# A hybrid decoder trunk on one core: norm weights as rows spread by a matmul, token tiles in other buffers, TensorE started on zeros

## The chip, the core and the metric

One core of a Trainium2 chip runs the whole program. The metric is the device time of one execution in microseconds; the profile is of one execution, recorded by the hardware profiler.

## The reference

A trunk of two layers over 1024 tokens of width 1024, in f32, with 256 memory tokens. What the change touches is the preparation: the RMSNorm of the memory tokens with the weights `g_mem`, the RMSNorm of the tokens with the weights `even_norm_g`, and the keys and values of the memory for both layers.

```
def rmsnorm(x, g):
    xf = x.astype(jnp.float32)
    y = xf * lax.rsqrt(jnp.mean(xf * xf, axis=-1, keepdims=True) + EPS)
    return (y * g.astype(jnp.float32)).astype(x.dtype)

mem_n = rmsnorm(mem, g_mem)                       # (256, 1024)
# even layer
h = rmsnorm(x, even_norm_g)                       # (1024, 1024)
proj = h @ w_in                                   # then attention, pooling, memory attention
mk, mv = jnp.split(mem_n @ w_mem_kv, 2, axis=-1)  # the same for the odd layer
```

After it come dilated window attention, pooling, memory attention, gating and an output projection (even layer), a spatial gate, memory attention and an output projection (odd layer), and a last norm.

## The kernel before, in words

Every large product is made in three matmuls of float32r operands: each f32 operand is split into a part `hi` (a copy on ScalarE, L113) and the rest `lo` (a subtraction on VectorE, L114). The projections use a seven-product scheme over blocks (`pair`, L236 is its matmul).

The change lies in the preparation. In program order it is:

- The two memory tiles of 128 tokens are loaded into buffers of the tag `xt` (three of them, L493), the weights `g_mem` are loaded with a broadcast to all 128 partitions into a buffer of the tag `gmb` (one, L496), and the identity for transposes (L497).
- `norm_T` for each memory tile: the square on ScalarE with its sum (L344), mean and epsilon on VectorE (L346), the power -1/2 on GpSimd (L347), the multiply by it and by the weights on VectorE (L372), eight transposes on TensorE (L377) into two PSUM banks (the first of the tag `s`, which has two banks, the other of `tr` or `pv`, one each), and from each bank a `hi` copy on ScalarE (L381) and a `lo` subtraction on VectorE (L382).
- The weights `g_even` are loaded with a broadcast into the same buffer `gmb` (L501).
- `mem_kv(0)` and `mem_kv(1)`: for each of four heads a weight tile is loaded (`mraw`, L505, six buffers) and split, 24 matmuls of 256 columns (L569) make the keys, the copy (L572) and the store (L573) follow; then one token tile is loaded (`xt`, L576) and goes through `norm_T` with `g_even`. Four more weight tiles and 48 matmuls of 512 columns (L402 to L404) make the values (copy L583, store L584). Between the two calls stands the table of rotation angles (`rope_angles`), which writes `sncs`.
- Then four weight tiles of the value projection are loaded into the buffers of the tag `raw` (three, L109), and the rest of the program follows.

All loads and stores go through SyncE's queue, in order. The order of each engine's instructions isn't written by hand: the framework takes the program's order as priority and places what it holds to be ready, when the program is built; so the order on an engine differs from that of the text (the load of L501 was issued behind two of L505 and one of L576). Buffers of one tag are used in turn, and a new use waits until the last reader of the old one is done.

Of the kernel before, what the change touches and what calls it, by code (L numbers as in the profile page):

```python
# [8 lines left out]
F32 = mybir.dt.float32  # L9
F32R = mybir.dt.float32r  # L10
BF = mybir.dt.bfloat16
I32 = mybir.dt.int32
AF = mybir.ActivationFunctionType
# [11 lines left out]
W2 = 10  # L25
# [24 lines left out]
def trunk(ctx, tc, A):  # L50
    nc = tc.nc
    PS = bass.MemoryType.PSUM
    V, S, G, T, D = nc.vector, nc.scalar, nc.gpsimd, nc.tensor, nc.sync

    def pool(name, side="left"):
        st = ExitStack()
        return st, st.enter_context(tc.tile_pool(name=name, bufs=1, side=side, reuse_waits="tile"))

    fix = ctx.enter_context(tc.tile_pool(name="fix", bufs=1))
# [3 lines left out]
    def bank(tag):  # L63
        return psum.tile([128, 512], F32, name=tag, tag=tag, bufs=dict(pj=4, s=2, tr=1, pv=1)[tag])
# [17 lines left out]
    def at(t, off, ap):  # L82
        return bass.AP(tensor=t.tensor, offset=t.offset + off, ap=ap)
# [7 lines left out]
    sncs = fix.tile([128, 2, 128], F32, name="sncs")  # L91
# [15 lines left out]
    def load_raw(src):  # L107
        raw = fix.tile([128, 1024], F32, name="raw", tag="raw", bufs=3)
        D.dma_start(raw, src)  # L109
        return raw  # L110
# [253 lines left out]
    def norm_T(*a):  # L364
        for _ in norm_steps(*a):
            pass
# [29 lines left out]
    def tok512(ps, hi_src, lo_src, chunks, t):  # L396
        ts = slice(t * 128, (t + 1) * 128)
        for k in range(8):
            wh, wl = chunks[k // 2]
            c = k % 2  # L400
            hi, lo = hi_src[k // 4][:, k % 4, ts], lo_src[k // 4][:, k % 4, ts]
            T.matmul(ps, hi, wh[c], start=(k == 0), stop=False)  # L402
            T.matmul(ps, hi, wl[c], start=False, stop=False)  # L403
            T.matmul(ps, lo, wh[c], start=False, stop=(k == 7))  # L404

    def bcast(ap, n, off=0):
        return bass.AP(tensor=ap.tensor, offset=ap.offset + off, ap=[[0, 128], [1, n]])
# [77 lines left out]
    sx, xn = pool("xn", "right")  # L485
# [1 line left out]
    mnh = [pm.tile([128, 4, 256], F32R, name=f"mnh{k}") for k in range(2)]  # L487
    mnl = [pm.tile([128, 4, 256], F32R, name=f"mnl{k}") for k in range(2)]
    mem_t = []
    gb = xn.tile([128, 1024], F32, name="gmb", tag="gmb")  # L490
    for t in range(2):
        m = xn.tile([128, 1024], F32, name="xt", tag="xt", bufs=3)
        D.dma_start(m, A["mem"][t * 128:(t + 1) * 128, :])  # L493
        mem_t.append(m)
        if t == 0:
            D.dma_start(gb, bcast(A["g_mem"], 1024))  # L496
            D.dma_start(ident, A["ident"])  # L497
    for t in range(2):
        norm_T(xn, mem_t[t], gb, mnh, mnl, t)
    gb2 = xn.tile([128, 1024], F32, name="gmb", tag="gmb")  # L500
    D.dma_start(gb2, bcast(A["g_even"], 1024))  # L501

    def m_raw(src):
        raw = p0.tile([128, 1024], F32, name="mraw", tag="mraw", bufs=MR)
        D.dma_start(raw, src)  # L505
        return raw

    def m_w(raw):
        o = []
        for c in range(2):  # L510
            hi = p0.tile([128, 4, 128], F32R, name="mwh", tag="mw", bufs=MW)
            lo = p0.tile([128, 4, 128], F32R, name="mwl", tag="mw", bufs=MW)
            f = "p k c -> p (k c)"
            split(raw[:, c * 512:(c + 1) * 512], hi.rearrange(f), lo.rearrange(f))
            o.append((hi, lo))
        return o

    def m_chunk(raw):
        o = m_w(raw)
        return [[x[q].rearrange("p k c -> p (k c)") for x in o] for q in range(2)]  # L520
# [41 lines left out]
    def mem_kv(l):  # L562
        for h in range(4):
            o = m_w(m_raw(A["kv1k" if l == 0 else "kv2k"][h]))
            ps = bank("pj")
            for k in range(8):
                hi, lo = o[k // 4]
                for w, m in ((hi, mnh), (hi, mnl), (lo, mnh)):
                    T.matmul(ps[:, :256], w[:, k % 4, :], m[k // 4][:, k % 4, :], start=(k == 0 and w is hi and m is mnh),  # L569
                             stop=(k == 7 and w is lo))  # L570
            mt = pm.tile([128, 512], F32, name="mt", tag="mt", bufs=2)
            S.activation(mt[:, :256], ps[:, :256], AF.Copy)  # L572
            D.dma_start(mkv_d[l, :, 0, h * 256:(h + 1) * 256], mt[:, :256])  # L573
            t = TORD[l * 4 + h]
            x = xn.tile([128, 1024], F32, name="xt", tag="xt", bufs=3)
            D.dma_start(x, A["x"][t * 128:(t + 1) * 128, :])  # L576
            norm_T(xn, x, gb2, hTh, hTl, t)
        ch = [m_chunk(m_raw(A["kv1v" if l == 0 else "kv2v"][c])) for c in range(4)]
        for t in range(2):
            ps = bank("pj")  # L580
            tok512(ps, mnh, mnl, ch, t)
            mt = pm.tile([128, 512], F32, name="mt", tag="mt", bufs=2)
            S.activation(mt, ps, AF.Copy)  # L583
            D.dma_start(mkv_d[l, :, 1, t * 512:(t + 1) * 512], mt)  # L584

    TORD = (4, 5, 6, 7, 0, 1, 2, 3)
    open_hT()
    mem_kv(0)
    D.dma_start(smalls, A["smalls"])
    rope_angles()  # L590
    mem_kv(1)
    ch = [chunk(p, A["wev"][c]) for c, p in enumerate((None, None, xn, xn))]
    sm.close()
# [6 lines left out]
    for t in TORD:  # L600
        ps = bank("pj")
# [709 lines left out]
```

## Time and profile before

| what | us |
|---|---|
| median of 3 runs | 1297.51 |
| lowest and highest run | 1295.16 and 1304.29 |
| the profiled execution | 1299.02 |
| its span | 1297.3 |

The span is the time from the first to the last instruction of the profile; the 1.7 us between it and the time of the same execution lie around it. Busy times are of instructions only; a matmul's own duration holds its way through the array, so matmuls that follow each other overlap, and their pace is read from the differences of their starts. L12 is line 12 of the kernel; L113, L114, L236, L344 to L382 are lines of helpers that many parts of the program use.

### The profile page before, as it was taken

Reading aid. Unit: us, or ns where it says so; the run is one execution under the profiler, and the core shown is the slowest. Engines: PE = TensorE matmul, PEld = TensorE weight load, DVE = VectorE, ACT = ScalarE, POOL = GpSimd, SP = SyncE. Lnnn points to the kernel's source line nnn. Section 1 sums busy time; section 2 is a strip of 40 time slices with the busy share of each in tenths; the row PEclk is TensorE's granted clock in tenths of the full one; section 3 lists DMA queues with packets and bytes.
Section 4 is the critical chain, followed back from the end, with each engine's and each line's share of the span. In section 5 each row is a group of like instructions: output and inputs, shape, how many; then the busy total and the mean of one; then the engine's idle time right before and its main releaser. Section 6 shows DMA issues by size and latency. Waiting matters only on the chain.

```text
span 1297.3 us, 17470 instructions
## 1 busy us (share of the span) xinstructions
PE 1255.0 (97%) x6008; PEld 1027.5 (79%) x6008; DVE 1042.8 (80%) x1968; ACT 576.7 (44%) x1155; POOL 48.3 (4%) x51
## 2 busy tenths in 40 slices
PE   6999999999999998999999999999999999999997
PEld 6888778878877776778888887877888877888886
DVE  6998768776776876879988977997878999777976
ACT  6734322232245455447653644632655233244552
POOL 1162000000000000000000001000000000000001
PEclk9999999999999999999999999998999999999999
DMA  7834756576555557633359534523122667239633
GB/s 273 281 98 142 216 189 205 189 241 198 162 161 181 159 172 259 224 114 94 122 177 373 164 114 188 185 90 114 34 83 97 212 217 252 66 106 334 243 112 130
DMA packets 128990, 226.10 MB, mean 174 GB/s; under 512 B 11139, under 2 KB 79363, under 8 KB 128902
## 3 DMA queue, kind: packets, MB, share of 16 engines
q1 hardware_dynamic: 128902, 224.99, 52.3%
q8 instruction: 47, 0.77, 0.3%
q14 instruction: 41, 0.34, 0.1%
HBM read 158.79 MB, written 63.01 MB: 171 GB/s over the span
## 4 chain that ended last, share of the span: by engine, by line
PE 72%; DVE 12%; DMA 10%; issue 3%; ACT 1%; POOL 1%; SPq 1%; DVEq 0%; POOLq 0%; ACTq 0%
PE pj L236 36%; DMA sl<-qk_d 3%; PE pj L954 3%; PE pj L953 3%; PE pj L955 3%; DVE wl L114 2%; PE pj L402 2%; PE pj L403 2%; PE pj L404 2%; PE pv L449 1%; PE pj L569 1%; PE s L430 1%; DMA raw<-in_we_dram 1%; PE s L720 1%; PE s L954 1%
## 5 line engine op out<-in xcount | busy, mean ns | idle before, releaser
L236 PE MATMUL pj<-hTh,wh 128*128 128x512 f32 x544 | 218.0, 401 | 8.7 <-DVE u L249 7.6
L236 PE MATMUL pj<-hTl,wh 128*128 128x512 f32 x544 | 215.1, 395 | 0.0
L236 PE MATMUL pj<-hTh,wl 128*128 128x512 f32 x544 | 214.5, 395 | 0.0
L113 ACT ACTIVATE wh<-sw 128x512 fp32r<-128x512 f32 x136 | 85.9, 632 | 244.6 <-PE pj L236 211.6
L236 PEld LDWEIGHTS pj<-hTh,wh 128*128 128x128 f32 x544 | 102.8, 189 | 36.5 <-DVE u L249 12.4
L113 ACT ACTIVATE wh<-raw 128x512 fp32r<-128x512 f32 x106 | 66.8, 630 | 142.9 <-PE pj L236 134.8
L114 DVE TENSOR_TENSOR wl<-sw,wh 128x512 fp32r<-128x512 f32 x136 | 93.6, 689 | 35.2 <-ACT wh L113 35.2
L236 PEld LDWEIGHTS pj<-hTh,wl 128*128 128x128 f32 x544 | 103.0, 189 | 21.5 <-issue 0.2
L236 PEld LDWEIGHTS pj<-hTl,wh 128*128 128x128 f32 x544 | 103.2, 190 | 19.8 <-issue 0.2
L113 ACT ACTIVATE owh<-raw 128x512 fp32r<-128x512 f32 x84 | 52.3, 628 | 73.8 <-DMA raw<-wt_d 31.5
L114 DVE TENSOR_TENSOR wl<-raw,wh 128x512 fp32r<-128x512 f32 x106 | 73.7, 696 | 9.4 <-ACT wh L113 8.1
L114 DVE TENSOR_TENSOR owl<-raw,owh 128x512 fp32r<-128x512 f32 x84 | 57.7, 691 | 29.1 <-ACT owh L113 28.5
L953 PE MATMUL pj<-owh,oyh 128*128 128x512 f32 x192 | 76.1, 397 | 0.0
L954 PE MATMUL pj<-owl,oyh 128*128 128x512 f32 x192 | 75.8, 395 | 0.0
L955 PE MATMUL pj<-owh,oyl 128*128 128x512 f32 x192 | 75.2, 395 | 0.0
L205 DVE TENSOR_TENSOR wt<-wt 128x256 f32<-128x256 f32 x128 | 51.7, 426 | 11.8 <-DMA wt<-in_wov_dram 5.2
L236 PE MATMUL pj<-t2h,wh 128*128 128x512 f32 x136 | 55.3, 407 | 0.0
L236 PE MATMUL pj<-t2l,wh 128*128 128x512 f32 x136 | 54.3, 399 | 0.0
L236 PE MATMUL pj<-t2h,wl 128*128 128x512 f32 x136 | 54.2, 399 | 0.0
L236 PE MATMUL pj<-t0h,wh 128*128 128x512 f32 x136 | 54.1, 398 | 0.0
L236 PE MATMUL pj<-t0l,wh 128*128 128x512 f32 x136 | 54.1, 398 | 0.0
L236 PE MATMUL pj<-t1l,wh 128*128 128x512 f32 x136 | 53.8, 395 | 0.0
(367 smaller groups left out, 3063.4 us busy)
## 6 DMA issues: line engine op xcount, KB each, us to landing
raw<-in_we_dram SPq DMA_DIRECT2D x44, 512.0 KB
wt_d<-wt SPq DMA_DIRECT2D x24, 512.0 KB
y<-y_d SPq DMA_DIRECT2D x24, 512.0 KB
raw<-wt_d SPq DMA_DIRECT2D x48, 256.0 KB
raw<-in_wo_dram SPq DMA_DIRECT2D x24, 512.0 KB
y_d<-X SPq DMA_DIRECT2D x20, 512.0 KB
qk_d<-X SPq DMA_DIRECT2D x24, 384.0 KB
sl<-qk_d SPq DMA_DIRECT2D x16, 512.0 KB
```

The lines of the kernel that those rows point to most:

```text
L113: S.activation(hi, raw, AF.Copy)
L114: e.tensor_tensor(lo, raw, hi.bitcast(F32), op=OP.subtract)
L205: V.tensor_tensor(tt[:, o, :], tt[:, x, :], tt[:, y, :], op=op)
L236: T.matmul(ps, w[:, k, :], m, start=(start and k == 0 and w is hi and m is B[k][0]), stop=(k == 3 and w is lo), skip_group_check=True)
L402: T.matmul(ps, hi, wh[c], start=(k == 0), stop=False)
L403: T.matmul(ps, hi, wl[c], start=False, stop=False)
L404: T.matmul(ps, lo, wh[c], start=False, stop=(k == 7))
L430: T.matmul(s3[:, a, :], qs[i][:, (t0 + a) * 128:(t0 + a + 1) * 128], kvp[j][:, :256], start=n == 0, stop=n == 2)
L449: T.matmul(pv[:, pr * 256:(pr + 1) * 256], kvp[i][:, 256 + kb * 128:384 + kb * 128], PT[j][:, kb * 256:(kb + 1) * 256], start=(kb == 0 and ...
L953: T.matmul(ps, yh[:, c], wh, start=start, stop=False, skip_group_check=True)
L954: T.matmul(ps, yh[:, c], wl, start=False, stop=False, skip_group_check=True)
L955: T.matmul(ps, yl[:, c], wh, start=False, stop=stop, skip_group_check=True)
```

## The change

The weights of the two norms come as rows of 4 KB into one partition of two buffers of the tag `raw`. A function `spread` multiplies a row by a row of ones (one partition of `sncs`, which is written later by the angles), in two matmuls of 512 columns into two banks of the tag `s`, and ScalarE copies the halves to the buffer `gmb`. A buffer of the tag `w2` is set to zero; `idle(n, tag)` issues n matmuls of 512 columns of these zeros, as bfloat16, into one bank: four ahead of the first spread and four behind it. The token tiles of numbers 0, 2 and 3 are loaded into buffers `raw` instead of `xt`.

```
--- before.py
+++ after.py
@@ -487,18 +487,38 @@
     mnh = [pm.tile([128, 4, 256], F32R, name=f"mnh{k}") for k in range(2)]
     mnl = [pm.tile([128, 4, 256], F32R, name=f"mnl{k}") for k in range(2)]
     mem_t = []
-    gb = xn.tile([128, 1024], F32, name="gmb", tag="gmb")
+
+    zero = fix.tile([128, 512], F32, name="zero", tag="w2", bufs=W2).bitcast(BF)
+    V.memset(zero, 0.0)
+    one = sncs[0:1, 0, :]
+    V.memset(one, 1.0)
+    grow = [fix.tile([128, 1024], F32, name="raw", tag="raw", bufs=3)[0:1, :] for _ in range(2)]
     for t in range(2):
         m = xn.tile([128, 1024], F32, name="xt", tag="xt", bufs=3)
         D.dma_start(m, A["mem"][t * 128:(t + 1) * 128, :])
         mem_t.append(m)
+        D.dma_start(grow[t], at(A[("g_mem", "g_even")[t]], 0, [[1024, 1], [1, 1024]]))
         if t == 0:
-            D.dma_start(gb, bcast(A["g_mem"], 1024))
             D.dma_start(ident, A["ident"])
+
+    def idle(n, tag):
+        ps = bank(tag)
+        for _ in range(n):
+            T.matmul(ps, zero[:, :128], zero[:, :512], start=True, stop=True)
+
+    def spread(row):
+        g = xn.tile([128, 1024], F32, name="gmb", tag="gmb")
+        for c in range(2):
+            ps = bank("s")
+            T.matmul(ps, one, row[:, c * 512:(c + 1) * 512], start=True, stop=True)
+            S.activation(g[:, c * 512:(c + 1) * 512], ps, AF.Copy)
+        return g
+    idle(4, "pj")
+    gb = spread(grow[0])
+    idle(4, "s")
     for t in range(2):
         norm_T(xn, mem_t[t], gb, mnh, mnl, t)
-    gb2 = xn.tile([128, 1024], F32, name="gmb", tag="gmb")
-    D.dma_start(gb2, bcast(A["g_even"], 1024))
+    gb2 = spread(grow[1])
 
     def m_raw(src):
         raw = p0.tile([128, 1024], F32, name="mraw", tag="mraw", bufs=MR)
@@ -572,8 +592,12 @@
             S.activation(mt[:, :256], ps[:, :256], AF.Copy)
             D.dma_start(mkv_d[l, :, 0, h * 256:(h + 1) * 256], mt[:, :256])
             t = TORD[l * 4 + h]
-            x = xn.tile([128, 1024], F32, name="xt", tag="xt", bufs=3)
-            D.dma_start(x, A["x"][t * 128:(t + 1) * 128, :])
+            n = l * 4 + h
+            if n in (0, 2, 3):
+                x = load_raw(A["x"][t * 128:(t + 1) * 128, :])
+            else:
+                x = xn.tile([128, 1024], F32, name="xt", tag="xt", bufs=3)
+                D.dma_start(x, A["x"][t * 128:(t + 1) * 128, :])
             norm_T(xn, x, gb2, hTh, hTl, t)
         ch = [m_chunk(m_raw(A["kv1v" if l == 0 else "kv2v"][c])) for c in range(4)]
         for t in range(2):
```

## Rows read from the trace of the kernel before

**Rows 1.** The page, part 1: busy us (share of the span) and instructions.

```profile
PE 1255.0 (97%) x6008; PEld 1027.5 (79%) x6008; DVE 1042.8 (80%) x1968; ACT 576.7 (44%) x1155; POOL 48.3 (4%) x51
```

**Rows 2.** Busy time by stretch: length, engines, granted clock, DMA share, GB/s.

```profile
0.00:15.00 15.00, 4.37 (x18) 3.44 (x18) 6.01 (x11) 8.40 (x14) 1.99 (x9) 1.00 0.75 245
15.00:24.30 9.30, 9.30 (x57) 9.21 (x58) 5.81 (x9) 5.24 (x11) 1.10 (x2) 1.00 0.80 294
24.30:60.00 35.70, 35.40 (x246) 31.88 (x244) 34.63 (x89) 25.64 (x51) 4.13 (x5) 1.00 0.85 296
8.00:10.00 2.00, 1.69 (x8) 1.57 (x8) 0.41 (x2) 1.32 (x3) 0.00 (x1) 1.00 1.04 424
```

**Rows 3.** The chain of waits, 0 to 60 us: start, us, what.

```profile
14.99 5.28 PE pj L569 x23
...
44.91 2.84 PE pj L569 x24
...
56.11 4.49 DMA raw<-in_wev_dram
```

**Rows 4.** Timeline of TensorE, 16 to 22 us: start, us, engine, line, what.

```profile
16.01 0.41 PE L569 MATMUL pj<-mnh,mwl 128*128 128x256 f32 x1
...
16.22 0.41 PE L569 MATMUL pj<-mnh,mwh 128*128 128x256 f32 x1
...
20.06 0.90 PE L377 MATMUL s<-ident,h 128*128 128x128 f32 x4
...
20.80 0.60 PE L377 MATMUL tr<-ident,h 128*128 128x128 f32 x4
...
21.83 0.29 PE L569 MATMUL pj<-mnh,mwl 128*128 128x256 f32 x1
...
21.95 0.28 PE L569 MATMUL pj<-mnh,mwh 128*128 128x256 f32 x1
```

**Rows 5.** Timeline of ScalarE and VectorE, 0 to 22 us.

```profile
4.90 1.06 ACT L344 ACTIVATE h<-xt 128x1024 f32<-128x1024 f32 x1 [2.82 <-DMA xt<-in_mem_dram]
...
6.97 1.29 DVE L372 SCALAR_TENSOR_TENSOR h<-xt,rs,gmb 128x1024 f32<-128x1024 f32 x1 [0.73 <-POOL rs L347]
...
8.58 1.06 ACT L344 ACTIVATE h<-xt 128x1024 f32<-128x1024 f32 x1 [2.53 <-DMA xt<-in_mem_dram]
...
10.59 1.28 DVE L372 SCALAR_TENSOR_TENSOR h<-xt,rs,gmb 128x1024 f32<-128x1024 f32 x1 [0.67 <-POOL rs L347]
...
14.25 0.68 DVE L382 TENSOR_TENSOR mnl<-s,mnh 128x512 fp32r<-128x512 f32 x1
...
16.44 1.28 DVE L372 SCALAR_TENSOR_TENSOR h<-xt,rs,gmb 128x1024 f32<-128x1024 f32 x1 [0.91 <-DMA gmb<-in_g_even_dram]
...
21.63 0.69 DVE L382 TENSOR_TENSOR hTl<-s,hTh 128x512 fp32r<-128x512 f32 x1 [0.53 <-ACT hTh L381]
```

**Rows 6.** Timeline of SyncE's queue, 0 to 12 us.

```profile
0.80 0.39 SPq L493 DMA_DIRECT2D xt<-in_mem_dram  x1
...
2.18 0.43 SPq L493 DMA_DIRECT2D xt<-in_mem_dram  x1
...
3.62 0.50 SPq L505 DMA_DIRECT2D mraw<-in_kv1k_dram  x1
11.90 0.33 SPq L501 DMA_DIRECT2D gmb<-in_g_even_dram  x1
```

**Rows 7.** Timeline, 395 to 400 us: a copy, a PSUM copy, f32 weight loads.

```profile
395.44 0.69 DVE L763 COPY PT<-tr 128x512 f32<-128x512 f32 x1 [1.99 <-PE tr L760]
...
398.10 0.60 ACT L771 ACTIVATE n<-pv 128x512 f32<-128x512 f32 x1
...
399.48 0.19 PEld L791 LDWEIGHTS tr<-ps,wp 128*128 128x128 f32 x1 [0.24 <-DVE st L690]
...
399.91 0.19 PEld L791 LDWEIGHTS tr<-ps,wp 128*128 128x128 f32 x1 [0.24 <-issue]
```

**Rows 8.** Line L1164, matmuls with two partitions: shortest, median, longest ns.

```profile
L1164 PE MATMUL pv<-rh,lh x16: 270/394/578, 892.7 to 897.6; 2*128 2x128 f32 x16
```

## The prediction

> **What bounds the kernel now.** I began with the page's busy times: TensorE has work in 97% of the span, VectorE in 80%, ScalarE in 44% [rows 1]. So only a stage in which TensorE is not the limit, or runs slowly, can give time back. The diff touches nothing after the preparation, so I read the table of busy time by stretch for the first 65 us [rows 2]. TensorE works 4.37 of the first 15.00 us, all of the next 9.30, 35.40 of 35.70 after that. The loss is at the start. From 24.3 to 60 us VectorE is as full as TensorE (34.63 of 35.70 us), so TensorE can be early there only by as much as VectorE is early too.
>
> Next came the chain of waits over the same 60 us [rows 3]. It runs through the load of the second memory tile (landed at 8.58 us), its norm, the subtractions of L382 and L114 on VectorE, and from 14.99 us through TensorE: 23 matmuls of L569 in 5.28 us. Further on the chain holds 24 of the same matmuls in 2.84 us. [...] The change of level falls between the transposes of 20.06 and of 20.80 us, after TensorE had worked without a pause from 14.99 us.
>
> The timeline of VectorE and ScalarE gives the other waits [rows 5]. The first norm's multiply (L372) runs at 6.97 us and waits for GpSimd, not for the weights. The second runs at 10.59 us, because its tile landed at 8.58 us. The first token tile's runs at 16.44 us and waited 0.91 us for the even norm's weights [rows 5]. Their load was issued at 11.90 us, since SyncE stood at it until the second multiply gave the only weight buffer back; every load behind it stood too, from 3.62 us on [rows 6].
>
> **The change part by part.** All sums are against the profiled execution, 1299.02 us with a span of 1297.3; it lies 1.5 us above the median of 1297.51, so I take differences from it and put them on the median.
>
> *The broadcast loads go.* Two loads of 512 KB leave the queue. The first stood before the second memory tile. Between 8 and 10 us the engines moved about 0.42 MB per us [rows 2]; 0.524 MB at that rate is 1.25 us, so the second tile lands at about 7.3 instead of 8.58 us. The second wait, of SyncE, goes as a whole.
>
> *What replaces them.* A 4 KB row each, a matmul per half with one partition, a copy per half. No row shows such a load's landing. From both sides: behind the first memory tile it takes no less than that tile (issued 0.80, used at 4.90 us: 4.1 us), at most what the second tile took (issued 2.18, used 8.58: 6.4 us) [rows 5, 6], so the row is there between 5.3 and 7.6 us; it sits right behind the first tile, and I take 5.3. Lower down, a row that passes the tile could be there at 3 us (a rival below).
>
> [...] The copy from PSUM is 0.60 us a half [rows 7].
>
> *First norm.* [...] The cover is the second tile: VectorE otherwise waits for it until 10.59 us. [...] So the earlier second tile pays for the later first norm, and this part is worth 0 (from -1.2 us, with the row early, to +2 us, if ScalarE's order puts both copies ahead of the first square).
>
> *The zeros.* One memset on VectorE costs between nothing and 0.69 us (a copy of 128x512) [rows 7]; VectorE has nothing to do until the first tile's square ends at 4.90 + 1.06 us [rows 5], which hides it; without that cover, 0.7. [...] Worth: 23 matmuls times (5.28/23 - 2.84/24) = 23 x 0.111 = 2.5 us, and of the 0.74 us that four transposes take from 20.06 to 20.80 us the higher level saves at most half, so 0.3: 2.8 us together [rows 3, 4].
>
> *The second spread.* [...] It needs two banks of the tag "s", which the subtractions of L382 give back, the second of them at 14.25 + 0.68 us [rows 5], and the weight buffer, free at 12.0. One half fits into the gap that TensorE has anyway before 14.99 us; the second starts when that bank is free, at about 14.5 us since the second tile's transposes are faster, and so delays L569 by about 0.4 us (bounds 0 and 1.7). [...]
>
> *Token tiles into other buffers.* The second token tile no longer waits behind L501: its load goes out some 8 us earlier. Before, no norm in the first 24 us waited for a token tile [rows 5], so I put nothing. The three tiles that use the buffers "raw" are read long before those are wanted again (L109, 56 us) [rows 3].
>
> Sum on TensorE up to the first token's transposes: -2.8 + 0.4 = -2.4 us; VectorE's end of that step (L382, 21.63 us [rows 5]) moves by as much, and its idle time between 15 and 24.3 us, 3.5 us [rows 2], has room for it. After that both engines go at their old pace, and the load at 56.11 us that TensorE waits for [rows 3] hangs on TensorE's own results, so it comes earlier as well. 1297.51 - 2.4 = 1295.1; I say 1295.
>
> [...]
>
> **The rivals.**
> *Everything early, 1292.7.* The row passes the tile and is there at about 3 us. Then the first norm isn't late, the second tile's 1.25 us count in full, the wait of 0.91 us goes, and the level is up before the transposes: 2.8 + 1.25 + 0.9 = 4.9 us. For it: the row is small. Against: the second tile's 6.4 us.
> [...]
> *VectorE keeps the gain, 1297.* From 24.3 us on it is 97% busy; if its splits before that come no earlier (they wait on ScalarE, not TensorE), TensorE's lead becomes a wait, and some 0.5 us is left. For it: rows 2. Against: 3.5 us of idle time on VectorE before.
>
> Beyond these the framework orders each engine's work anew, and an instruction placed elsewhere may be worth 1 to 2 us either way (single waits in [rows 5] are 0.5 to 0.9 us); that widens the range.
>
> **How the numbers follow.** Forecast 0.46, early 0.18, low level 0.18, VectorE 0.18. All four lie within 1% (13 us), which is about what a measurement of this kernel can tell from no change; even TensorE's whole idle time of the first 15 us, 10.6 us [rows 2], is less. For chance differences and the unknown order I leave 0.03 faster and 0.04 slower. The range runs from the early case less 2 us to the slow case and a little more, 1290.5 to 1301; the forecast's own is 1293.5 to 1296.5.
>
> **What would show it.** Right: L569 at 0.12 us spacing from its first matmul; the first norm's multiply near 9.4 us and the second still ending near 12; the first token's multiply near 16; its transposes near 17.7 instead of 20.06; a constant shift of some 2.4 us from 24 us to the end. Wrong: L569 at 0.21 us; the copies of the first spread ahead of the first square on ScalarE; VectorE waiting more than before in 24 to 60 us; the shift gone by 65 us.

## The result and the profile after

| | median us | lowest and highest |
|---|---|---|
| before, 8 runs beside the changed kernel | 1298.72 | 1294.82 and 1304.29 |
| after, 8 runs | 1306.84 | 1300.70 and 1310.03 |

The ratio of after to before is 1.006 with a 95% interval of 1.0039 to 1.0081: the change makes the kernel slower, by 5.1 to 10.5 us on 1298.7. Within 1% is right, 1295 is not, and the upper end of the range, 1301, was too low. The profiled execution is the longest of the eight, 1310.03 us with a span of 1308.3.

The page of after, part 1, answers to [rows 1]:

```profile
PE 1267.5 (97%) x6024; PEld 1029.4 (79%) x6024; DVE 1042.9 (80%) x1970; ACT 579.9 (44%) x1159; POOL 46.4 (4%) x51
```

TensorE is busy 12.5 us longer than in [rows 1], with 16 instructions more; VectorE is not. Busy time by stretch of after, with the columns of [rows 2]:

```profile
0.00:15.00 15.00, 11.84 (x29) 5.65 (x30) 5.35 (x9) 7.41 (x12) 1.44 (x8) 1.00 0.86 318
15.00:24.30 9.30, 9.30 (x33) 6.12 (x32) 5.26 (x9) 5.07 (x10) 1.10 (x2) 1.00 0.01 3
24.30:60.00 35.70, 34.21 (x240) 31.10 (x239) 31.86 (x80) 27.12 (x55) 4.11 (x5) 1.00 0.81 279
```

In the first 15 us TensorE is now busy 11.84 us; the 7.47 us more are in the main the zeros (2 x 1.89) and the first spread (3.74). In the next 9.3 us it issues 33 instructions instead of 57. VectorE does 0.66 us less work in the first stretch, 0.55 us less in the second and 2.77 us less in the third, where it was nearly as full as TensorE; so some 4 us of its work are pushed out behind 60 us. The DMA share from 15 to 24.3 us falls from 0.80 to 0.01.

TensorE's timeline of after (start, us, engine, line, what, idle before and what ended it); L507 are the zeros, L513 the spreads, L589 the key matmuls that were L569:

```profile
1.52 1.89 PE L507 MATMUL pj<-zero 128*128 128x512 bf16 x4 [1.52 <-DVE zero L492]
4.66 3.74 PE L513 MATMUL s<-raw,sncs 1*128 1x512 f32 x4 [1.25 <-DMA raw<-in_g_mem_dram]
8.34 1.89 PE L507 MATMUL s<-zero 128*128 128x512 bf16 x4
10.48 1.12 PE L377 MATMUL s<-ident,h 128*128 128x128 f32 x4 [0.26 <-DVE ss L346]
...
13.46 1.06 PE L377 MATMUL pv<-ident,h 128*128 128x128 f32 x4
14.46 2.07 PE L513 MATMUL s<-raw,sncs 1*128 1x512 f32 x2
16.46 0.58 PE L589 MATMUL pj<-mnh,mwh 128*128 128x256 f32 x1
16.97 2.07 PE L513 MATMUL s<-raw,sncs 1*128 1x512 f32 x2
18.97 0.58 PE L589 MATMUL pj<-mnl,mwh 128*128 128x256 f32 x1
...
21.48 0.41 PE L589 MATMUL pj<-mnh,mwh 128*128 128x256 f32 x1
21.70 0.41 PE L589 MATMUL pj<-mnl,mwh 128*128 128x256 f32 x1
21.91 1.05 PE L377 MATMUL s<-ident,h 128*128 128x128 f32 x4
...
26.84 0.39 PE L589 MATMUL pj<-mnh,mwl 128*128 128x256 f32 x1 [0.90 <-DVE mwl L114]
...
29.01 0.63 PE L377 MATMUL s<-ident,h 128*128 128x128 f32 x4 [0.49 <-DVE h L372]
```

The first transposes take 1.12 and 1.06 us against the 0.60 at 20.80 us in [rows 4], and the key matmuls are 0.22 us apart (21.48 to 21.70) against 0.12 at 22 us there. The low and the high level are these two paces, here and below: key matmuls 0.21 to 0.22 or 0.12 us apart, four transposes in 1.01 to 1.12 or in 0.60 to 0.66 us. So the level is still the low one, though the granted clock of these stretches reads 1.00, as it did before. That the paces at the start are levels of the clock is thus the author's reading; in e2 below a lower granted clock does stand beside the low pace. The second spread takes 2.07 us a half, with one key matmul between the halves, so the row of key matmuls that began at 14.99 us [rows 3] begins at 18.97. The first token's transposes come at 21.91 instead of 20.06 us. Two waits on VectorE follow, 0.90 and 0.49 us.

VectorE of after, against [rows 5]:

```profile
9.14 1.28 DVE L372 SCALAR_TENSOR_TENSOR h<-xt,rs,gmb 128x1024 f32<-128x1024 f32 x1 [3.29 <-ACT gmb L514]
11.15 1.28 DVE L372 SCALAR_TENSOR_TENSOR h<-xt,rs,gmb 128x1024 f32<-128x1024 f32 x1 [0.67 <-POOL rs L347]
...
19.76 1.28 DVE L372 SCALAR_TENSOR_TENSOR h<-raw,rs,gmb 128x1024 f32<-128x1024 f32 x1 [3.21 <-issue]
```

ScalarE's copies of the second spread in the same trace:

```profile
16.62 0.60 ACT L514 ACTIVATE gmb<-s 128x512 f32<-128x512 f32 x1 [0.43 <-PE s L513]
19.08 0.60 ACT L514 ACTIVATE gmb<-s 128x512 f32<-128x512 f32 x1 [1.86 <-PE s L513]
```

The memory norms are where the forecast had them. The first token's multiply is not: VectorE stands idle for 3.21 us before it. The profile writes "issue" there, but ScalarE's copy of the second half of the weights ends at 19.08 + 0.60 = 19.68 us, just before 19.76. In e9 below, with the same spread, the profile names that copy for the same multiply. So the second spread holds TensorE's key matmuls and VectorE's next norm at the same time.

SyncE's queue of after, against [rows 6]:

```profile
8.80 0.43 SPq L525 DMA_DIRECT2D mraw<-in_kv1k_dram  x1
24.95 0.33 SPq L593 DMA_DIRECT2D mkv_d<-mt  x1
```

The same store in the kernel before:

```profile
20.71 0.33 SPq L573 DMA_DIRECT2D mkv_d<-mt  x1
```

The next thing in the queue is the store of the first keys, and it waits for those keys until 24.95 us; all later loads stand behind it. That is the empty DMA stretch. The emptiness by itself is no loss: the weight and token loads that went out from 12.32 to 13.70 us before are out by 8.80 us here. What is late is the store and with it the loads behind it, by 4.24 us.

TensorE's start times, the same matmul in both traces, are 4.4 us later at 40 to 58 us, 4.7 at 95 to 118, 7.4 at 176 to 205. The second step lies in the first projections. VectorE of after there:

```profile
129.51 2.14 DVE L205 TENSOR_TENSOR wt<-wt 128x256 f32<-128x256 f32 x5 [2.62 <-DMA wt<-in_wov_dram]
...
133.90 0.68 DVE L249 TENSOR_TENSOR u<-pj,m 128x512 f32<-128x512 f32 x1
```

And TensorE of after right behind them:

```profile
134.64 0.50 PE L236 MATMUL pj<-hTh,wh 128*128 128x512 f32 x1 [1.25 <-DVE u L249]
```

The same line of VectorE in a second trace of the kernel before (the run "before again" below):

```profile
122.25 2.14 DVE L205 TENSOR_TENSOR wt<-wt 128x256 f32<-128x256 f32 x5 [0.87 <-DMA wt<-in_wov_dram]
```

VectorE waits 2.62 instead of 0.87 us for a weight load, the sum L249 stands behind it on VectorE, and TensorE waits 1.25 us for L249, a wait that the trace of before does not have there. This second step belongs to this trace: in that of e1 below, after without its zeros, the same wait is 0.79 us.

```profile
125.23 2.14 DVE L205 TENSOR_TENSOR wt<-wt 128x256 f32<-128x256 f32 x5 [0.79 <-DMA wt<-in_wov_dram]
```

### The profile page after: what moved, and what is told of

Its sections match the earlier page's. It is cut to its first block, busy times and chain, and to the rows that moved or that the text cites. A ratio compares the mean times of both kernels' runs of the same rounds, so it can differ in the third digit from the quotient of the medians.

```text
span 1308.3 us, 17511 instructions
## 1 busy us (share of the span) xinstructions
PE 1267.5 (97%) x6024; PEld 1029.4 (79%) x6024; DVE 1042.9 (80%) x1970; ACT 579.9 (44%) x1159; POOL 46.4 (4%) x51
## 4 chain that ended last, share of the span: by engine, by line
PE 64%; DVE 15%; DMA 14%; issue 3%; ACT 1%; SPq 1%; POOL 1%; DVEq 0%; POOLq 0%; ACTq 0%
PE pj L236 30%; DMA sl<-qk_d 3%; DVE wl L114 3%; PE pj L979 2%; DMA raw<-in_we_dram 2%; PE pj L978 2%; PE pj L977 2%; PE s L744 2%; PE pj L403 1%; PE pj L404 1%; DMA raw<-in_wo_dram 1%; PE pj L402 1%; PE s L430 1%; PE pv L449 1%; DMA ws_d<-wt 1%
## 5 line engine op out<-in xcount | busy, mean ns | idle before, releaser
L236 PE MATMUL pj<-t0h,wl 128*128 128x512 f32 x136 | 54.2, 399 | 0.0
L236 PE MATMUL pj<-t1h,wl 128*128 128x512 f32 x136 | 53.6, 394 | 0.0
```

Source lines behind the costliest of these rows:

```text
L236: T.matmul(ps, w[:, k, :], m, start=(start and k == 0 and w is hi and m is B[k][0]), stop=(k == 3 and w is lo), skip_group_check=True)
```

## The experiments

Every ratio is to runs of the kernel before on the same chip. The last two columns are the median shift of TensorE's starts against the first profile of before, in us.

| run | ratio | 95% interval | 40 to 58 us | 176 to 205 us |
|---|---|---|---|---|
| after | 1.0060 | 1.0039 to 1.0081 | +4.4 | +7.4 |
| e1 after without zeros | 1.0052 | 1.0032 to 1.0072 | +3.4 | +3.0 |
| e9 before, second spread alone | 1.0055 | 1.0031 to 1.0080 | +2.2 | +3.9 |
| e2 after, second weights loaded | 1.0004 | 0.9984 to 1.0023 | +0.4 | +2.1 |
| e15 as e2, no zeros | 1.0006 | 0.9988 to 1.0025 | +0.8 | +1.8 |
| e10 before, second spread early | 0.9994 | 0.9976 to 1.0011 | -2.6 | -2.6 |
| e11 before, second weights loaded early | 1.0004 | 0.9988 to 1.0021 | -0.9 | -0.7 |
| e3 before, token tiles in raw | 1.0008 | 0.9992 to 1.0023 | -0.7 | +0.1 |
| e6 before, buffers turned | 1.0003 | 0.9984 to 1.0022 | -0.7 | -0.6 |
| e5 before again | 0.9995 | 0.9977 to 1.0013 | -0.6 | -0.5 |
| e4, e12 before, eight zeros | 1.0039, 1.0040 | 1.0020 to 1.0058, 1.0018 to 1.0062 | 0.0, -0.4 | +0.5, +0.3 |
| e13 as e4, eight columns each | 1.0039 | 1.0019 to 1.0059 | -0.7 | -0.6 |
| e14 before, four zeros | 1.0013 | 0.9997 to 1.0029 | -0.2 | +0.1 |
| e7 before, sixteen of ones | 1.0047 | 1.0030 to 1.0064 | -0.4 | +5.6 |
| e8 before, sixteen of zeros | 1.0056 | 1.0028 to 1.0084 | +0.1 | +7.5 |

**After without the zeros (e1).**

```
-    V.memset(zero, 0.0)
...
-    idle(4, "pj")
     gb = spread(grow[0])
-    idle(4, "s")
```

> The changed kernel without the zeros: no memset, no matmuls of zeros; both spreads and the token buffers stay. Theory A (the second spread costs): the key matmuls still start near 19 us at a spacing of 0.21 us, 60 to 110 us into the run TensorE is 4.5 to 5.5 us behind the kernel before, and the ratio to it stays at 1.005 to 1.007. Rival B (the zeros cost, by their time on TensorE or by what they do to the clock): the lag at 60 us falls below 2 us and the ratio to 1.002 or less.

1.0052: the loss stays, so the zeros are not its bulk; it lies 0.0008 below after, and with intervals 0.4% wide it cannot say more of them. TensorE's delay was smaller than expected, 3.4 us at 40 to 58 us and 2.3 at 95 to 118, and it did not grow to 205 us (3.0); yet the time is some 7 us over that of the kernel before.

**After with the second weights by a broadcast load (e2), and that without zeros (e15).**

```
...
-    gb2 = spread(grow[1])
+    gb2 = xn.tile([128, 1024], F32, name="gmb", tag="gmb")
+    D.dma_start(gb2, bcast(A["g_even"], 1024))
```

> The changed kernel with the second weights (even norm) loaded by the broadcast of before instead of spread; zeros, first spread and token buffers stay. Theory A (the second spread stands on TensorE ahead of the key matmuls, four passes of 0.85 us at the low clock, and makes the first token's norm wait): the key matmuls start near 15.5 us, the lag at 60 us is 0 to 1.5 us, the ratio 1.000 to 1.002. Rival C (the buffers: rows and tokens in 'raw' shift what later stages use): the lag at 60 us goes but a lag of 3 us or more grows later, ratio 1.003 or more.

> The kernel with the second weights by a broadcast load (first by row and spread, tokens in other buffers), now without its zeros; with them it measured 1.0004. If the zeros, in two portions of four as the change has them, cost what they cost alone: 0.995 to 0.998. If in two portions they cost nothing: 0.9985 to 1.002.

1.0004 and 1.0006. Taking away the second spread gives the whole loss back, with the first spread, the tokens' buffers and the zeros still there. TensorE's timeline of e2 (L590 key matmuls):

```profile
10.75 1.01 PE L377 MATMUL tr<-ident,h 128*128 128x128 f32 x4
11.95 0.63 PE L377 MATMUL s<-ident,h 128*128 128x128 f32 x4 [0.19 <-DVE h L372]
...
13.97 0.39 PE L590 MATMUL pj<-mnh,mwh 128*128 128x256 f32 x1 [0.96 <-ACT mnh L381]
...
15.06 0.41 PE L590 MATMUL pj<-mnh,mwh 128*128 128x256 f32 x1
15.27 0.41 PE L590 MATMUL pj<-mnl,mwh 128*128 128x256 f32 x1
```

Here the level comes up between the second and the third group of transposes (1.01 to 0.63 us). Behind a wait of 0.96 us the first key matmul still takes 0.39 us, where it takes 0.58 in after, but from 15.06 us on they are 0.21 us apart: the level is down again, and here the granted clock is lower too: 0.87 from 12 to 16 us and 0.70 from 16 to 20 us. The zeros do something at this place: the first token's transposes come at 19.89 us here and at 21.54 in e15. At 40 to 58 us 0.4 us of that is left, and the time is the same with and without them; so in the two portions of the change they cost and bring nothing that shows in the time.

**The tokens' buffers alone (e3).**

```
+            n = l * 4 + h
+            if n in (0, 2, 3):
+                x = load_raw(A["x"][t * 128:(t + 1) * 128, :])
```

> The kernel before with the token tiles 0, 2 and 3 in the buffers 'raw' and nothing else. Theory A: the same time as before within 1.5 us (ratio 0.999 to 1.001), as no norm of the first 24 us waited for a token tile. Rival C (the buffers cost later): ratio 1.003 or more, the lag growing after 110 us.

1.0008, an interval that holds 1: nothing, as forecast.

**The kernel before again (e5), and before with one buffer of `w2` taken by a memset (e6).** The first measures the comparison itself. The second shifts which buffer each later user of the tag gets, as the change does too.

> The kernel before, unchanged, as one more kernel beside itself: what two equal programs differ by. Ratio 0.999 to 1.001, and a lag of TensorE against the first profile that wanders by 1 to 3 us after 110 us although every engine's order is the same. If that holds, lags below 3 us in one profile say nothing. Rival: the lag stays within 0.3 us to the end, and then the lags of the experiments after 110 us are theirs.

> The kernel before with one memset of a tile of the tag 'w2' ahead of all else and no matmul of it: the ten buffers of the split weights are handed out one further on for the whole run. Rival C (the turned buffers cost later): as the kernel with zeros alone, some 2 to 5 us slower, ratio 1.002 to 1.004. Otherwise (the zeros' matmuls or chance): ratio 1.000 within 0.001.

0.9995 and 1.0003. The comparison tells 0.2% apart. It also tells how far one profile may be trusted: the trace of e5 is that of the same kernel, and TensorE is 0.6 us ahead of the first trace up to 147 us, 2.9 at 520 to 560 us and 7.0 at 1120 to 1200 us. Shifts are read here up to 205 us and no further.

**The second spread alone, in the kernel before (e9).** The weights `g_mem` stay a broadcast load; no zeros.

```
-    gb2 = xn.tile([128, 1024], F32, name="gmb", tag="gmb")
-    D.dma_start(gb2, bcast(A["g_even"], 1024))
+    gb2 = xn.tile([128, 1024], F32, name="gmb", tag="gmb")
+    for c in range(2):
+        ps = bank("s")
+        T.matmul(ps, one, grow[:, c * 512:(c + 1) * 512], start=True, stop=True)
+        S.activation(gb2[:, c * 512:(c + 1) * 512], ps, AF.Copy)
```

> Before with one part alone: the even norm's weights come as a row and are spread by two matmuls behind the memory norms; the memory norm's weights stay a broadcast load, no zeros, token tiles as before. Theory A (the second spread at the low clock, ahead of and among the key matmuls, makes the change slower): the two spread matmuls take about 2 us each between 14 and 19 us, key matmuls up to 4 us later than before, first token's transposes some 1 to 2 us later; TensorE 2 to 5 us behind at 58 us and more than half of the change's excess in the time: 1.002 to 1.006. Rival (the first spread, or both spreads together with their order, makes it): within 0.2% of before.

1.0055, the excess of the whole change by one part. TensorE's timeline of e9 (L508 spread, L577 key matmuls):

```profile
13.00 1.06 PE L377 MATMUL pv<-ident,h 128*128 128x128 f32 x4
13.99 2.07 PE L508 MATMUL s<-raw,sncs 1*128 1x512 f32 x2
15.99 0.58 PE L577 MATMUL pj<-mnh,mwh 128*128 128x256 f32 x1
16.50 2.07 PE L508 MATMUL s<-raw,sncs 1*128 1x512 f32 x2
18.50 0.58 PE L577 MATMUL pj<-mnl,mwh 128*128 128x256 f32 x1
```

The same picture as in after: two halves of 2.07 us around the first key matmul, the rest from 18.50 us on instead of 14.99. VectorE of e9 waits for the second copy:

```profile
19.30 1.28 DVE L372 SCALAR_TENSOR_TENSOR h<-xt,rs,gmb 128x1024 f32<-128x1024 f32 x1 [1.36 <-ACT gmb L509]
```

The runs of e9 have a mean granted clock of 0.9950, those of the kernel before beside them 0.9948; so its loss is no lower clock in mid-run. The framework orders the first 74 us of e9 anew as well, TensorE's work included; but e2, e15 and e10 are ordered anew too and lose nothing. The first token's transposes come at 23.42 us, 3.4 later than before, where 1 to 2 were expected.

**The same spread at an early place (e10).** The row of `g_even` is the first load of the queue, the spread stands ahead of both memory norms, and `g_mem` is loaded by broadcast into a buffer `raw`, so that `gmb` is free.

```
+    D.dma_start(grow, at(A["g_even"], 0, [[1024, 1], [1, 1024]]))
     for t in range(2):
         m = xn.tile([128, 1024], F32, name="xt", tag="xt", bufs=3)
...
+    for c in range(2):
+        ps = bank("s")
+        T.matmul(ps, one, grow[:, c * 512:(c + 1) * 512], start=True, stop=True)
+        S.activation(gb2[:, c * 512:(c + 1) * 512], ps, AF.Copy)
     for t in range(2):
         norm_T(xn, mem_t[t], gb, mnh, mnl, t)
```

> The same spread at another place: the even norm's weights are the first load of the queue, spread ahead of both memory norms while TensorE has nothing to do, into the weight buffer, while the memory norm's weights are loaded into a buffer of the row tag. Theory A (the place costs, not the spread): spread ends before 8 us, key matmuls begin at 15 us or earlier, the first token's multiply does not wait for weights, TensorE at 58 us between 2 us ahead and 1 us behind, ratio 0.997 to 1.001. Rival (a spread costs wherever it stands, by its order on ScalarE or what the framework makes of it): 1.003 to 1.006.

0.9994. The spread has the same length as in after (3.75 us for both halves), and costs nothing there; e11 below has most of the other parts of this edit without it. TensorE's timeline of e10 (L505 spread, L576 key matmuls):

```profile
2.31 3.75 PE L505 MATMUL s<-raw,sncs 1*128 1x512 f32 x4 [2.31 <-DMA raw<-in_g_even_dram]
10.03 1.09 PE L377 MATMUL s<-ident,h 128*128 128x128 f32 x4 [3.98 <-DVE ss L346]
...
14.34 0.39 PE L576 MATMUL pj<-mnh,mwh 128*128 128x256 f32 x1 [0.30 <-ACT mnh L381]
15.07 0.39 PE L576 MATMUL pj<-mnl,mwh 128*128 128x256 f32 x1 [0.34 <-DVE mnl L382]
15.29 0.28 PE L576 MATMUL pj<-mnh,mwl 128*128 128x256 f32 x1
15.41 0.27 PE L576 MATMUL pj<-mnh,mwh 128*128 128x256 f32 x1
...
17.90 0.60 PE L377 MATMUL s<-ident,h 128*128 128x128 f32 x4
```

The key matmuls run 0.12 us apart from 15.29 us, and the first token's transposes come at 17.90 instead of 20.06 us. This is the picture of the forecast, in another kernel. TensorE stays 2.6 us ahead to 205 us, so VectorE did not take this gain back there, and the time's interval (-3.1 to +1.4 us) holds that gain as well as none. So no version here is shown to be faster than the kernel before.

**The second weights loaded early (e11).** As e10, with a broadcast load behind the second memory tile in place of row and spread.

```
+        if t == 1:
+            gb2 = xn.tile([128, 1024], F32, name="gmb", tag="gmb")
+            D.dma_start(gb2, bcast(A["g_even"], 1024))
```

> Before, with the even norm's weights loaded by broadcast right behind the second memory tile, into the weight buffer, and the memory norm's weights into a buffer of the row tag: SyncE no longer stands, no spread, no zeros. If the stand of SyncE and the wait of 0.91 us were worth something: 0.997 to 0.999. If they were hidden, as the tokens in other buffers were: 0.999 to 1.001. If the 0.5 MB ahead of the first weight tiles matters: 1.001 to 1.002.

1.0004: the stand of SyncE and the wait of 0.91 us [rows 5, 6] were hidden.

**Eight zeros ahead of the first transposes (e4, and once more as e12), four (e14), and eight with eight columns each (e13).** They change nothing but these matmuls and the memset.

```
...
+    idle(4, "pj")
+    idle(4, "s")
     for t in range(2):
         norm_T(xn, mem_t[t], gb, mnh, mnl, t)
```

> The kernel before with the eight matmuls of zeros ahead of the first transposes (they run from about 1.5 to 5 us) and nothing else. Theory A (these zeros don't bring the clock up by the time of the key matmuls): spacing still 0.21 us from 15 us on, time as before within 1 us. Forecast's step (zeros bring the clock up): spacing 0.12 us from the first key matmul, 2.5 us less. Rival B (the zeros cost): 2 us or more slower.

> The kernel with the eight zeros alone once more, unchanged (1.0039 the first time, with no delay that the trace shows up to 147 us). If the zeros themselves cost: 1.002 to 1.006 again. If the first comparison was high by chance, since the same kernel in the full change made no difference against the one without zeros that its interval shows: 0.999 to 1.002.

> Zeros alone, four matmuls of 512 columns instead of eight, in one row ahead of the first transposes, as the change has them there. If the price grows with the work in one row: 1.001 to 1.003; if it is there with any zeros at all: 1.003 to 1.005; if it takes more than the change puts in one row: 0.999 to 1.001.

> The kernel with zeros alone, the same sixteen TensorE instructions at the same place, but eight columns in each matmul instead of 512, so some 3 us less work for the array. If the array's early work makes the 1.004 (through the clock that is granted later): 0.999 to 1.001. If it is the added instructions themselves (how the stream is fetched, what stands where): 1.003 to 1.005 again.

TensorE's timeline of e4 (L503 zeros):

```profile
1.52 1.89 PE L503 MATMUL pj<-zero 128*128 128x512 bf16 x4 [1.52 <-DVE zero L492]
3.20 1.91 PE L503 MATMUL s<-zero 128*128 128x512 bf16 x4
8.46 1.12 PE L377 MATMUL s<-ident,h 128*128 128x128 f32 x4 [3.35 <-DVE h L372]
```

Eight zeros in a row and then a wait of 3.35 us: the transposes behind it take 1.12 us, the low level. They measured 1.0039 and 1.0040, yet the trace shows no delay up to 147 us. Eight columns instead of 512 leave the price as it was (1.0039); with four the interval holds 1. Part of the 5 us goes with the granted clock of the whole run: its mean is 0.9926 in e4 and 0.9932 in e12, against 0.9954 and 0.9948 in the runs of the kernel before beside them. At 1.1 us for 0.001 (last section) that is an estimated 3 and 2 us; in e13 (0.9943 against 0.9952) it is 1 us. What lowers the clock, and where the rest lies, no profile shows; the profiled execution of e13, with a span of 1295.0 us, doesn't even have the loss. This stays open. It is no part of the change's loss as far as e2 and e15 can tell.

**Sixteen matmuls ahead of the first transposes, of ones (e7) and of zeros (e8).**

```
+    zero = sncs.rearrange("p a c -> p (a c)").bitcast(BF)
+    V.memset(zero, 1.0)
...
+    idle(16, "pj")
```

> The kernel before with sixteen matmuls of ones (bfloat16, 512 columns, from a tile that is written later anyway, so no buffers turn) ahead of the first transposes, 1.5 to 8.4 us. If the level of the clock rises on matmuls whose data switch: key matmuls 0.12 us apart from 15 us on, first token's transposes near 17.5 instead of 20.06, lag at 60 us -1.5 to -2.8, ratio 0.998 to 0.999. If the transposes in between let it fall again: spacing 0.21 us and no gain. The zeros' kernel beside it tells whether the data matter.

> The same with sixteen matmuls of zeros. If only the time that TensorE is at work matters: as with ones. If the data matter: spacing still 0.21 us at 15 us, no gain, while the ones gain. If the eight zeros were only too few: spacing 0.12 us in both.

TensorE's timeline of e7 (L503 ones, L577 key matmuls):

```profile
1.52 6.56 PE L503 MATMUL pj<-sncs 128*128 128x512 bf16 x16 [1.52 <-DVE sncs L492]
8.30 0.66 PE L377 MATMUL s<-ident,h 128*128 128x128 f32 x4 [0.22 <-DVE h L372]
...
11.98 0.66 PE L377 MATMUL s<-ident,h 128*128 128x128 f32 x4 [2.58 <-DVE h L372]
...
14.43 0.58 PE L577 MATMUL pj<-mnl,mwh 128*128 128x256 f32 x1 [0.73 <-DVE mnl L382]
14.81 0.41 PE L577 MATMUL pj<-mnh,mwl 128*128 128x256 f32 x1
15.02 0.41 PE L577 MATMUL pj<-mnh,mwh 128*128 128x256 f32 x1
...
18.74 0.60 PE L377 MATMUL s<-ident,h 128*128 128x128 f32 x4
```

Behind sixteen of them, zeros as well as ones, the first transposes are at the high level (0.66 us). It doesn't last: behind a wait of 2.58 us the transposes still take 0.66 us, but behind a further one of 0.73 us a key matmul takes 0.58 us, and from 14.81 us they are 0.21 us apart again. The first token's transposes come 1.3 us earlier than before, 18.74 against 20.06 us, but at 40 to 58 us only 0.4 of that is left, and at 176 to 205 us TensorE is 5.6 us late. The framework had ordered the preparation anew for these sixteen, so the time, 1.0047, can't be read as what the early high level is worth. The mean granted clock is lower here too (0.9918 in e7 and 0.9902 in e8, against 0.9948), by the same estimate 3 and 5 of the 6 and 7 us. The slow start of the kernel before, up to 20 us, reads 1.00, so it lowers no such mean.

## Why the prediction was wrong, point by point

**What held.** The start is where the loss and the room lie, and a part's price is read from its stage. The row landed right behind the first memory tile: TensorE waited for it until 4.66 us, where 5.3 was taken. The first norm's multiply came at 9.14 us (9.4 forecast), the second ended at 11.15 + 1.28 = 12.43 (12.0), 0.56 us behind the 11.87 of before, where this part was put at 0. The tokens' buffers were worth nothing (e3). The two calls of a spread are busy 3.74 us at the low level, 2.07 us a half behind the norms. Behind the first tile the row was waited for until 4.66 us, as first load (e10) until 2.31 us. The order of landing is not always that of issue: in e2 the wait for the row ended at 4.02 us, and the square of the tile ahead of it began at some 4.4 us (an estimate: VectorE takes the square's sum at 5.58 us; in e9 it does at 5.61 us, 1.18 us behind the square's start at 4.43).

**The step that failed first: "L569 at 0.12 us spacing from its first matmul".** The spacing was 0.21 to 0.22 us. The 2.8 us of the sum take the high level from the first transposes on, and no run with the change's zeros shows it there: the first group takes 1.12 us in after, 1.11 in e2 and 1.12 in e4. In [rows 3, 4] the level rose after work without a pause from 14.99 us. Such work was not sufficient here: after has it from 4.66 to 21.9 us with two breaks of 0.26 us or less, and the key matmuls at 21.7 us are still at the low level. In e2, with the same zeros and first spread, the level was up at the third group of transposes (11.95 us, 0.63 us). What decides between the two is not shown by these traces. Nor would the level from the zeros have been enough: in e2 it fell again behind the next waits, and without zeros (e15) the time was the same.

**The step that made the time: "The second spread ... delays L569 by about 0.4 us (bounds 0 and 1.7)".** It delayed it by 18.97 - 14.99 = 3.98 us. The step hung on the first one: the 0.4 us, with a second half that starts at 14.5, need a half of some 0.9 us (an estimate), and no run shows one; at the low level each half is 2.07 us. The gap that was to hold the first half was gone when the transposes ended, at 14.46 us, so both halves lie on the path. VectorE's multiply came at 19.76 us, where 16 was forecast. The low level, with its chance of 0.18 and the sign "L569 at 0.21 us", is the case that came. The range gives it at most 1301, a price that no run shows: the row of L569 alone moved by 3.98 us, and VectorE stood 3.21 us behind ScalarE's second copy. The single runs settle that this part at this place makes the loss: this part alone 1.0055, the change without it 1.0004, the part at an early place 0.9994. How much of it comes by TensorE's late row and how much by VectorE's late norm they do not separate.

**The step that failed last: "After that both engines go at their old pace".** The loads hang on SyncE's queue, the queue on the store of the first keys, and the store on TensorE: 24.95 instead of 20.71 us, the same 4.2 us. In the trace of after the loads behind it, and the wait for `wt` at 129 us, go with a shift of 7.4 us at 176 to 205 us, so there the late start was not only kept but enlarged. That the late loads and not another consequence of the shift make this second step was read from the waits and not tried by itself. Nor is it needed for the loss: e1 has no such step (3.4 us at 40 to 58 us, 3.0 at 176 to 205), e9 a small one (2.2 and 3.9), and their times are some 7 us over all the same. So at 205 us about half of the loss of these two stands in the trace, and how a start 4 us late comes to some 7 us at the end stays open.

**VectorE as the end of any gain.** The rival "VectorE keeps the gain" fits e7, where TensorE is 1.3 us early at 19 us and 0.4 at 40 to 58 us, but its order is another. In e10 it does not hold: 2.2 us early at 18 us, 2.6 at 40 to 58 and at 176 to 205 us.

## What to carry to other kernels

A small operation that stood between two stages was priced here at the pace that TensorE had there, and on all the engines that waited for its result; as its input could be there early, the place of it was worth more than its length (two halves of 2.07 us cost some 7 us at 14 us, 4 to 10 by the interval of e9, and nothing at 2.3 us). Matmuls put in to raise the level can lose it again before the work that is to profit: in e2 and e7 the level fell around waits of 0.96 us and of 2.58 and 0.73 us, while in e10 the key matmuls behind waits of 0.30 and 0.34 us go on 0.12 us apart. A late store held the loads behind it in SyncE's queue (24.95 instead of 20.71 us, the next load at 25.38 instead of 21.13), so look at a delay again at the first stage that waits for a load.

## What was not expected of the hardware

- Behind sixteen matmuls of zeros (e8) the level is up as behind sixteen of ones (e7): in both the first transposes take 0.66 us. After waits of 2.40 to 2.58 us and then of 0.62 to 0.73 us it was down again.
- The level stayed the low one (key matmuls 0.22 us apart at 21.48 us) through 17 us in which TensorE was busy but for some 0.4 us (after, 4.66 to 21.9 us).
- The granted clock falls for some microseconds in mid-run in the profiles of before, after, e10, e13 and e14 (stretches of 5 us at 0.50 to 0.96) and not in that of e11 (1.00 up to 1285 us). One place recurs but not always: 165 to 185 us is granted 0.91 in the traces of before and of after, 170 to 180 us 0.82 and 0.84 in that of e13 and 0.93 and 0.73 in that of e14, and 1.00 in that of e11. Over all runs a mean granted clock lower by 0.001 goes with some 1.1 us more: of 126 runs of the kernel before the twelve longest (1300.5 to 1303.3) had 0.991 to 0.993, the twelve shortest (1289.3 to 1293.2) 0.995 to 0.999. That is about half of the variance from run to run.
- Eight more matmuls ahead of the first transposes made 1.004, with 512 columns each as with 8; a lower mean granted clock goes with part of it, and no profile shows a place for the rest.
